# Sixteen rows of zeros on the store queue ahead of a streaming L1 normalisation

## The chip, the core and the metric

The kernel runs on one core of one Trainium2 chip. The metric is device time in microseconds (us), the median of repeated executions; lower is better. Engines are named as in the profile: DVE is VectorE, ACT is ScalarE, POOL is GpSimd, SP is SyncE, PE is TensorE (not used here). "q1" is the DMA queue on which SP issues transfers, "q10" the one on which ACT issues them.

## What is computed

Each row of 1024 floats is divided by the sum of its absolute values plus a tiny constant. There are 32 x 512 = 16384 rows, 67.1 MB in and as much out.

```python
def setup_inputs():
    batch, seq, dim = 32, 512, 1024
    return {"x": np.random.randn(batch, seq, dim).astype(np.float32)}

def reference(x):
    sums = np.sum(np.abs(x), axis=-1, keepdims=True)
    return (x / (sums + 1e-8)).astype(np.float32)
```

## The kernel before

The input is seen as 16384 rows of 1024 elements, and cut into eleven tiles (the list `rows`, line 34). A tile lies over 128 partitions, with twelve rows in each partition (48 KB of a partition, 6 MB in all); the last tile has eight rows per partition (32 KB, 4 MB in all). The function `piece` (lines 36 to 43) says where a tile lies in memory: tiles 0, 1 and the last one share the first 4096 rows of the tensor, 32 consecutive rows per partition, of which tile 0 has the first twelve, tile 1 the next twelve and the last tile the last eight. Tiles 2 to 9 are blocks of 1536 consecutive rows.

Tiles live in a pool of four buffers (`BUFS`, line 45), so that up to four are in flight. The result is written over the input in the same buffer, and stored from there. A second pool, `stats`, holds the row sums and their reciprocals.

For each tile the loop (lines 86 to 91) does the following. SP issues the load (line 88). DVE reduces the absolute values along each row (line 52), adds the constant (line 59) and takes the reciprocal (line 61). Then the rows are multiplied: most of them by one DVE multiplication with the reciprocal broadcast (line 63), in a few tiles some rows by single DVE instructions (line 70) and some by ACT (line 73). The table `split` says how many rows go to the second and third way. Last, ACT issues the store of the tile (line 91). There are eleven loads on q1 and eleven stores on q10.

The body stands in a manual schedule: every engine executes its own instructions in the order in which the program writes them, and the framework adds the semaphore waits that the data call for. A load into a buffer waits until the store that used this buffer before has landed; so load 4 waits for store 0. On SP there is nothing but loads, on ACT multiplications and stores alternate, and on DVE each tile's instructions follow those of the tile before.

Of the kernel before, what the change touches and what calls it, by code (L numbers as in the profile page):

```python
# [1 line left out]

# [4 lines left out]

FP32 = mybir.dt.float32
EPS = 1e-8


@with_exitstack
def kernel(
    ctx: ExitStack,
    tc: tile.TileContext,
    x: bass.AP,
    out: bass.AP,
):
    nc = tc.nc
    P = nc.NUM_PARTITIONS  # L20

    x_flat = x.flatten_outer_dims()
    out_flat = out.flatten_outer_dims()
    n, d = x_flat.shape

    R = 12
    BUFS = 4  # L30
    HEAD = 32
    per_partition = n // P
    assert n % P == 0 and (per_partition - HEAD) % R == 0
    rows = [R] * ((per_partition - HEAD) // R + 2) + [HEAD - 2 * R]

    def piece(flat, i):
        head = flat[: P * HEAD, :].rearrange("(p r) d -> p r d", p=P)
        if i < 2:
            return head[:, R * i : R * (i + 1), :]
        if i == len(rows) - 1:  # L40
            return head[:, 2 * R :, :]
        a = P * (HEAD + R * (i - 2))
        return flat[a : a + P * R, :].rearrange("(p r) d -> p r d", p=P)

    sbuf = ctx.enter_context(tc.tile_pool(name="sbuf", bufs=BUFS))
    stats = ctx.enter_context(tc.tile_pool(name="stats", bufs=len(rows)))

    def normalize(x_tile, k, kv, kt):


        s = stats.tile([P, R], FP32)
        nc.vector.tensor_reduce(  # L52
            out=s[:, :k],
            in_=x_tile[:, :k, :],
            axis=mybir.AxisListType.X,
            op=mybir.AluOpType.add,
            apply_absolute_value=True,
        )
        nc.vector.tensor_scalar_add(out=s[:, :k], in0=s[:, :k], scalar1=EPS)  # L59
        inv = stats.tile([P, R], FP32)  # L60
        nc.vector.reciprocal(out=inv[:, :k], in_=s[:, :k])  # L61
        if kv:
            nc.vector.tensor_mul(  # L63
                out=x_tile[:, :kv, :],
                in0=x_tile[:, :kv, :],
                in1=inv[:, :kv].unsqueeze(2).to_broadcast([P, kv, d]),
            )
        for r in range(kv, kv + kt):
            row = x_tile[:, r, :]
            nc.vector.tensor_scalar_mul(out=row, in0=row, scalar1=inv[:, r : r + 1])  # L70
        for r in range(kv + kt, k):
            row = x_tile[:, r, :]
            nc.scalar.activation(  # L73
                out=row,
                in_=row,
                func=mybir.ActivationFunctionType.Copy,
                scale=inv[:, r : r + 1],
            )

    last = len(rows) - 1
    split = {0: (3, 4), 1: (0, 3), 2: (0, 3), last - 1: (0, 2), last: (5, 3)}

    with tc.manual_schedule():
        for i, k in enumerate(rows):
            x_tile = sbuf.tile([P, R, d], FP32)
            nc.sync.dma_start(out=x_tile[:, :k, :], in_=piece(x_flat, i))  # L88
            kt, ks = split.get(i, (0, 0))
            normalize(x_tile, k, k - kt - ks, kt)  # L90
            nc.scalar.dma_start(out=piece(out_flat, i), in_=x_tile[:, :k, :])


# [1 line left out]
_INS = ['x']  # L95
_OUTS = [((32, 512, 1024), 'float32')]


# [23 lines left out]
```

## Time and profile before

| | us |
|---|---|
| median of 3 runs | 316.94 |
| lowest and highest | 316.83, 317.59 |
| span of the profiled execution | 315.80 |
| DVE busy in that span | 261.2 (83%) |
| ACT busy | 17.4 (6%) |
| bytes read and written | 67.11 MB each, 425 GB/s over the span |

The profile is of one execution; its span goes from the first to the last instruction on the core, and the page gives that execution no other time. The page divides the span into 40 slices and gives the busy share of each engine in tenths; the line "DMA" there is the mean share of the core's 16 DMA engines. The windows of the trace give the same for any stretch, with the bytes moved. The list of DMA queues can be asked for any stretch too: it then counts the packets that began in it, their megabytes, and the time that these packets took as a share of 16 engines over the stretch, which can so be over 100%. One packet of data is what one partition contributes to a transfer.

The costliest groups of instructions, with count, busy time and mean duration:

| line, engine | what | count | busy us | mean ns |
|---|---|---|---|---|
| 52 DVE | sum of absolute values, 128x12288 | 10 | 129.5 | 12950 |
| 63 DVE | multiplication, 128x12288 | 6 | 77.8 | 12958 |
| 73 ACT | multiplication of one row per partition, 128x1024 | 15 | 16.1 | 1138 |
| 70 DVE | the same on DVE, 128x1024 | 8 | 5.5 | 748 |

A load of 6 MB takes 38.0 us from issue to landing in the median (16.9 for the first, 80.6 at most), a store 47.4 us; the last store, of 4 MB, 20.6 us.

### The profile page before, as it was taken

Reading aid. Unit: us, or ns where it says so; the run is one execution under the profiler, and the core shown is the slowest. Engines: PE = TensorE matmul, PEld = TensorE weight load, DVE = VectorE, ACT = ScalarE, POOL = GpSimd, SP = SyncE. Lnnn points to the kernel's source line nnn. Section 1 sums busy time; section 2 is a strip of 40 time slices with the busy share of each in tenths; the row PEclk is TensorE's granted clock in tenths of the full one; section 3 lists DMA queues with packets and bytes.
Section 4 is the critical chain, followed back from the end, with each engine's and each line's share of the span. In section 5 each row is a group of like instructions: output and inputs, shape, how many; then the busy total and the mean of one; then the engine's idle time right before and its main releaser. Section 6 shows DMA issues by size and latency. Waiting matters only on the chain.

```text
span 315.8 us, 168 instructions
## 1 busy us (share of the span) xinstructions
DVE 261.2 (83%) x51; ACT 17.4 (6%) x16; POOL 0.2 (0%) x4
## 2 busy tenths in 40 slices
DVE  0079999999999999969996999799699969999200
ACT  0010404004000000000000000000000000201200
POOL 0000000000000000000000000000000000000000
DMA  8999999999999999999999999999999999999986
GB/s 324 473 398 448 448 361 430 405 486 405 405 486 405 405 486 411 423 467 405 448 436 411 479 405 411 473 417 405 473 417 411 467 413 450 421 442 423 473 374 282
DMA packets 3168, 134.22 MB, mean 425 GB/s; under 512 B 352, under 2 KB 352, under 8 KB 352
## 3 DMA queue, kind: packets, MB, share of 16 engines
q1 hardware_dynamic: 1584, 67.11, 49.8%
q10 hardware_dynamic: 1584, 67.11, 49.1%
HBM read 67.11 MB, written 67.11 MB: 425 GB/s over the span
## 4 chain that ended last, share of the span: by engine, by line
DVE 41%; DMA 33%; another core or an unknown queue 18%; issue 0%; SPq 0%; DVEq 0%
DVE s L52 23%; DMA x_tile<-in_x_dram 17%; DMA out_dram<-x_tile 16%; DVE x_tile L63 15%; DVE x_tile L70 1%; DVE inv L61 0%; DVE s L59 0%; SPq L88 0%; DVEq L117 0%
## 5 line engine op out<-in xcount | busy, mean ns | idle before, releaser
L52 DVE TENSOR_REDUCE s<-x_tile 128x12 f32<-128x12288 f32 (+1 forms) x11 | 138.2, 12561 | 31.5 <-DMA x_tile<-in_x_dram 31.5
L63 DVE TENSOR_TENSOR x_tile<-x_tile,inv 128x12288 f32<-128x12288 f32 (+3 forms) x10 | 113.6, 11358 | 0.5
L73 ACT ACTIVATE x_tile<-x_tile,inv 128x1024 f32<-128x1024 f32 x15 | 16.1, 1138 | 258.7 <-DVE inv L61 258.7
L70 DVE TENSOR_SCALAR x_tile<-x_tile,inv 128x1024 f32<-128x1024 f32 x8 | 5.5, 748 | 0.0
L61 DVE RECIPROCAL inv<-s 128x12 f32<-128x12 f32 (+1 forms) x11 | 2.5, 226 | 0.4
L73 ACT ACT_TABLE_LOAD x1 | 1.3, 1283 | 17.7 <-DMA x_tile<-in_x_dram 17.7
L59 DVE TENSOR_SCALAR s<-s 128x12 f32<-128x12 f32 (+1 forms) x11 | 1.9, 173 | 0.4
L106 POOL MEMSET const-bfloat16-1.0<- 128x1 bf16 x1 | 0.1, 102 | 0.0
L106 POOL MEMSET const-uint8-127<- 128x1 uint8 x1 | 0.1, 102 | 0.0
L106 POOL MEMSET const-float32-0.0<- 128x1 f32 x1 | 0.1, 99 | 0.2 <-issue 0.2
L106 POOL MEMSET const-float32-1.0<- 128x1 f32 x1 | 0.1, 99 | 0.0
## 6 DMA issues: line engine op xcount, KB each, us to landing
x_tile<-in_x_dram SPq DMA_DIRECT2D x10, 6144.0 KB, 38.0
out_dram<-x_tile ACTq DMA_DIRECT2D x10, 6144.0 KB, 47.4
x_tile<-in_x_dram SPq DMA_DIRECT2D x1, 4096.0 KB, 33.3
out_dram<-x_tile ACTq DMA_DIRECT2D x1, 4096.0 KB, 20.6
```

Of the source, the lines that this page charges most:

```text
L52: nc.vector.tensor_reduce(out=s[:, :k], in_=x_tile[:, :k, :], axis=mybir.AxisListType.X, op=mybir.AluOpType.add, apply_absolute_value=True,)
L59: nc.vector.tensor_scalar_add(out=s[:, :k], in0=s[:, :k], scalar1=EPS)
L61: nc.vector.reciprocal(out=inv[:, :k], in_=s[:, :k])
L63: nc.vector.tensor_mul(out=x_tile[:, :kv, :], in0=x_tile[:, :kv, :], in1=inv[:, :kv].unsqueeze(2).to_broadcast([P, kv, d]),)
L70: nc.vector.tensor_scalar_mul(out=row, in0=row, scalar1=inv[:, r : r + 1])
L73: nc.scalar.activation(out=row, in_=row, func=mybir.ActivationFunctionType.Copy, scale=inv[:, r : r + 1],)
L106: nc = _bacc.Bacc("TRN2", target_bir_lowering=False, num_devices=1)
```

## The change

A small tile of zeros, 16 partitions of 128 floats, is filled by DVE, and ACT issues a transfer that writes it to the result: 512 bytes into the beginning of 16 different rows, the first row of the last tile in each of its first 16 partitions. The last tile's store writes all of these places again at the end. The loop is rewritten into functions for load, computation and store; the first four loads are written ahead of the loop, and load i + 4 behind store i.

```diff
+    tiles = {}
+
+    def load(i):
+        x_tile = tiles[i] = sbuf.tile([P, R, d], FP32, name="x_tile")
+        nc.sync.dma_start(out=x_tile[:, : rows[i], :], in_=piece(x_flat, i))
+
+    def store(i):
+        nc.scalar.dma_start(out=piece(out_flat, i), in_=tiles[i][:, : rows[i], :])
+
+    def compute(i):
+        k = rows[i]
+        kt, ks = split.get(i, (0, 0))
+        normalize(tiles[i], k, k - kt - ks, kt)
+
     with tc.manual_schedule():
-        for i, k in enumerate(rows):
-            x_tile = sbuf.tile([P, R, d], FP32)
-            nc.sync.dma_start(out=x_tile[:, :k, :], in_=piece(x_flat, i))
-            kt, ks = split.get(i, (0, 0))
-            normalize(x_tile, k, k - kt - ks, kt)
-            nc.scalar.dma_start(out=piece(out_flat, i), in_=x_tile[:, :k, :])
+        zero = ctx.enter_context(tc.tile_pool(name="zero", bufs=1)).tile([16, 128], FP32, name="zero")
+        nc.vector.memset(zero, 0.0)
+        nc.scalar.dma_start(out=piece(out_flat, len(rows) - 1)[:16, 0, :128], in_=zero)
+        for i in range(BUFS):
+            load(i)
+        for i in range(len(rows)):
+            compute(i)
+            store(i)
+            if i + BUFS < len(rows):
+                load(i + BUFS)
```

## The prediction

> **What bounds the kernel now.** I read the busy slices first, then the table of windows, the waits and the timeline, and last the DMA queues in single microseconds.
>
> ```profile
> DVE  0079999999999999969996999799699969999200
> DMA  8999999999999999999999999999999999999986
> q1 hardware_dynamic: 1584, 67.11, 49.8%
> q10 hardware_dynamic: 1584, 67.11, 49.1%
> ```
>
> The 16 DMA engines are busy in every slice; VectorE starts late and has holes. q1 (SP's loads) and q10 (ACT's stores) share those engines half and half. Of 3168 packets 352 are under 512 B (completion marks), so 2816 carry data, 176 per engine: 160 of 48 KB (a partition's twelve rows) and 16 of 32 KB (eight rows).
>
> ```profile
> 120.00:140.00 20.00, 18.04 (x4) 0.00 (x0) 0.00 (x0) 1.00 1.00 435
> 40.00:60.00 20.00, 19.90 (x4) 3.23 (x3) 0.00 (x0) 1.00 1.02 415
> 0.00:2.00 2.00, 0.00 (x0) 0.00 (x0) 0.20 (x4) 1.00 1.10 344
> ```
>
> The columns are window, length, busy DVE, ACT and POOL, clock, DMA share and GB/s. The rate is 435 in the middle and 415 in the window in which the first store joins: 20 GB/s for 20 us is 0.40 MB, or 0.9 us of transfer lost there.
>
> ```profile
> DVE s L52 <- DMA x_tile<-in_x_dram: 31.5, 7, 17.6
> 140.72 12.95 DVE L52 TENSOR_REDUCE s<-x_tile 128x12 f32<-128x12288 f32 x1 [2.51 <-DMA x_tile<-in_x_dram]
> 38.67 0.38 ACTq L91 DMA_DIRECT2D out_dram<-x_tile  x1
> ```
>
> VectorE waits for loads, 17.6 us before the first and some 2.5 us before each of the later ones; nobody waits long for VectorE except ACT, whose share is small. So the end is set by how much work each DMA engine has, and by nothing else that I can find. The third row is the first store: issued at 38.67 us, the first use of q10.
>
> The single microseconds show where the 0.9 us went. A packet is counted where it starts and the share is of 16 engines, so share x 16 / packets is the duration of one.
>
> ```profile
> q1 hardware_dynamic: 14, 0.69, 220.9%
> ...
> q1 hardware_dynamic: 16, 0.79, 181.5%
> ...
> q1 hardware_dynamic: 15, 0.74, 170.6%
> ...
> q1 hardware_dynamic: 16, 0.79, 307.9%
> ...
> q10 hardware_dynamic: 15, 0.74, 170.2%
> ```
>
> These are the microseconds from 1, 4, 38, 40 and 43. The very first packets take 2.209 x 16 / 14 = 2.52 us. Later ones take 1.815 us (1.815 x 16 / 16), and those of 38 us 1.82. At 40 us, just before q10's first packets start, one packet on every engine takes 3.079 us: 1.26 us too long. q10's first packets themselves (43 us) take 1.815. Both queues hold work from then on (a load takes 38.0 us to land and the next is issued after some 29), so no row shows what a restart after a pause would cost. **The stall of 1.26 us per engine belongs to q10's first use, and it falls where the engines have no slack.** Check of the sum: 160 x 1.815 + 16 x 1.21 (by bytes) = 309.8; plus 1.7 us before the first packet, 0.70 for the long first packets and 1.26 for the stall gives 313.5, beside a span of 315.8 in which the transfers die out in the 314th microsecond.
>
> **The change part by part.** All sums stand against the span of 315.80; the median of the runs is 316.94, 1.14 us more, and I carry that over unchanged, since the page gives the profiled execution no time of its own.
>
> *The order of the Python loop: 0.* Loads, computation and stores are now written as functions, and four loads come ahead of the loop. SP issues nothing but loads, in the same order, each still behind the store that frees its buffer; VectorE and ACT keep their orders too. Loads 0 to 3 already leave together in the trace (SP's four issues span 0.73 to 2.62 us). Load 4 leaves at 74.08 because store 0 (38.67 + 35.3) has landed by then, and it still must.
>
> *The memset: 0 to 0.2 us, hidden.* POOL's memsets of 128x1 take 0.10 us, VectorE's add on 128x12 0.17. VectorE has nothing to do until 17.65 us; that wait hides it. Without this cover it would cost 0.2 us once. Queued behind it on ACT is only the zero store, for which it must wait; what is next on ACT waits for load 0 at 17.70 us anyway.
>
> *The 16 rows of zeros: 0.02 us per engine by their bytes.* If the rows are spread over the engines, each gets 512 B, and 512 / 49152 x 1.815 = 0.02 us. The other end is one whole packet's time, 1.8 us, if an engine is held as long by a small packet as by a large one. I take the small end, since the rate follows bytes in all rows above, and keep the other for the range.
>
> [...]
>
> *The last store must come after the zeros: 0.* Only store 10 overwrites them, at 294.08 us. The zeros should land within some microseconds of the start, so an added wait on ACT is long met; queued behind it is nothing but the end. Were the wait put on store 0 at 38.67 it would be met as well.
>
> *The first use of q10 moves to the head: from -1.26 to +1.26 us.* When does it come? Load 0 is issued at 0.73 and its first packets start in the microsecond from 1, by the 2-us window around 1.7: about 1.0 us of lag. The zero store can be issued after the memset, 0.73 + 0.2, so by the same lag q10's rows reach the engines at about 1.9 us. There the engines do no full work: the first q1 packets run 2.52 - 1.82 = 0.70 us longer than normal. If q10's start is served in that waiting time, 0.70 of the 1.26 is hidden in any case, and all of it if it begins before data flows. The gain then lies between 0.70 - 0.02 = 0.68 and 1.26 - 0.02 = 1.24; I take the middle, 1.0.
>
> [...] The trace's own lag of 1.0 us is what I use.
>
> What is late next? If the head loses up to 1.26 us, load 0 and VectorE's start move from 17.65 to at most 18.9. VectorE runs without a gap until 111.17, then waits 0.57 us for load 4 and 2.51 us before the reduction at 140.72. A delay of 1.26 us is gone by that second wait, and q10 is never empty meanwhile (store 2, issued at 84.92, takes 47.1 us, and store 3 leaves at 111.19). VectorE passes nothing of it on.
>
> **The rivals.**
>
> *Forecast, the stall is hidden at the head:* 316.94 - 1.0 = 315.9. For it: the stall is seen once, and the engines wait at the head anyway. Against it: at 40 us q1 had packets waiting and could not fill the stall, so an engine may stop as a whole.
>
> *The stall only moves:* engines stop 1.26 us at about 4 us, when load 0's first packets are through, instead of at 40. -1.26 + 1.26 + 0.02 gives 316.96, no change. It decides if the zeros reach the engines after load data flows, which is 0.2 us away by my working. For it: the same argument about whole engines.
>
> *The stall is not prepaid (slower):* it belongs to the first large store, not to the queue, and stays at 40 us; the zeros pay one more at the head. +1.26 + 0.02 gives 318.2. It is decided by what a 512 B packet leaves behind in an engine. For it: no row shows a small packet preparing a large one, and neither queue has a pause after its start in which a cost of restarting could be seen. Against it: both queues go over 67 MB of new addresses afterwards with packets of 1.815, so it isn't new addresses that cost the time.
>
> *The change does nothing at all* (an ordering wait holds the zeros back until late): then q10 starts at 38.67 as before and the time is 316.94; it goes with the second case.
>
> **How the numbers follow.** Hidden at the head 0.43, moved or without effect 0.33, not prepaid 0.24. A difference of 0.3% is 0.95 us, about what measurement can tell from no change: 315.99 and 317.89 are the marks. The first case holds gains from 0.68 to 1.24 and is on the faster side in most of its span; a few partial gains fall to "same" and a few from the second case come out faster. So faster 0.41, same 0.35, slower 0.24. The time is that of the likeliest case, 315.9; its own range is 315.6 to 316.3. The range goes from 315.4 (the whole 1.24 and the 0.3 us by which repeated runs differ) to 318.1, which holds nearly all of the second case and part of the third.
>
> **What would show it.** In the changed kernel's trace the packets of the 40th microsecond should take 1.815 us and not 3.08; the window from 40 to 60 should reach some 435 GB/s; q10's first packets should stand near 2 us, the load packets after them should take 2.5 us and no more, and VectorE should start at 17.65 or at most 0.5 later. If packets near 4 us take 3 us and VectorE starts near 18.9, the stall has moved. If 3.08 is still there at 40 us, it was not prepaid. The prediction is wrong if the stall has another cause than q10's first use, or if small packets hold an engine for a microsecond.

## The result and the profile after

The changed kernel takes 317.78 us in the median of 20 runs, beside 317.22 us for 20 runs of the kernel before: a ratio of 1.0016, 95% interval 1.001 to 1.0023. It is slower by 0.56 us in the medians, some 0.2%. Compared once more (12 and 23 runs) it gave 317.57 beside 317.20, ratio 1.0015 (0.9999 to 1.0031), an interval that just reaches 1. The forecast was 1.0 us faster.

The page of the changed kernel, with its two new rows:

```profile
span 316.1 us, 170 instructions
DVE  0079999999999999969996997899699969999100
DMA  8999999999999999999999999999999999999986
q1 hardware_dynamic: 1584, 67.11, 49.7%
q10 hardware_dynamic: 1616, 67.12, 49.0%
L96 DVE MEMSET zero<- 16x128 f32 x1 | 0.2, 165 | 0.8 <-PEq L119 0.8
out_dram<-zero ACTq DMA_DIRECT2D x1, 8.0 KB, 7.5
```

The picture is the old one. q10 has 32 packets more, 16 of zeros and, between 7 and 9 us, 16 of under 512 B, as many as each of the 22 transfers has in the page of before (352); the zeros land 7.5 us after their issue. The stretches and the waits that the prediction read, in the changed kernel's windows, its waits and its timeline:

```profile
40.00:60.00 20.00, 19.90 (x4) 3.23 (x3) 0.00 (x0) 1.00 1.02 413
120.00:140.00 20.00, 17.73 (x4) 0.00 (x0) 0.00 (x0) 1.00 1.00 435
...
DVE s L47 <- DMA x_tile<-in_x_dram: 29.9, 7, 16.6
...
38.65 0.36 ACTq L85 DMA_DIRECT2D out_dram<-x_tile  x1
```

The window in which the first store joins still moves 413 GB/s beside 435 (415 before). VectorE starts at 17.62 us (17.65 before) and the first store leaves at 38.65 (38.67). Now the DMA queues of the changed kernel in the microseconds from 1, from 4, from 5 to 7 (two rows), from 40 and from 43; again the share x 16 x the window's length / packets is one packet's time:

```profile
q1 hardware_dynamic: 15, 0.74, 235.9%
...
q1 hardware_dynamic: 16, 0.79, 181.5%
...
q1 hardware_dynamic: 16, 0.79, 90.8%
q10 hardware_dynamic: 16, 0.01, 1.4%
...
q1 hardware_dynamic: 16, 0.79, 309.8%
...
q10 hardware_dynamic: 15, 0.74, 170.2%
```

The zeros run from 5 to 7 us, each for 1.4% x 16 x 2 / 16 = 0.03 us, and the load packets beside them take the normal 1.816. At 40 us the packets take 309.8% x 16 / 16 = 3.10 us, as they did before (3.08). **The stall was neither prepaid nor moved, and q10's first use shows no cost in the packets.** So the transfer explains no gain, and the loss has to be looked for elsewhere.

The loss is in two other places. The first is the close of the program, where all five engines have drains and semaphore waits. These are the rows of the generated closing code from 314.6 us on, four of each kernel, first in the kernel before, then in the changed one (engine, count, duration in ns, first and last start):

```profile
L117 SPq DRAIN  x3: 7/7/7, 314.9 to 315.2; - x3
L117 DVEq EVENT_SEMAPHORE  x2: 21/21/21, 315.1 to 315.8; - x2
L117 ACTq DRAIN  x1: 8/8/8, 315.2 to 315.2; - x1
L117 DVEq DRAIN  x1: 19/19/19, 315.3 to 315.3; - x1
```

```profile
L130 SPq DRAIN  x3: 7/7/7, 315.0 to 315.3; - x3
L130 DVEq EVENT_SEMAPHORE  x2: 21/21/21, 315.2 to 316.1; - x2
L130 ACTq DRAIN  x1: 8/8/8, 315.3 to 315.3; - x1
L130 DVEq DRAIN  x1: 143/143/143, 315.8 to 315.8; - x1
```

Before, VectorE drains at 315.3 us, with ScalarE, and only its very last wait is late: the trace has it at 315.78 us, where the other engines have theirs at 315.59 to 315.60. In the changed kernel the drain itself comes at 315.76, 0.44 us behind ScalarE's (315.32), and the others wait for it: the last waits of SyncE and ScalarE come at 316.05 and 316.06. From SyncE's drain ahead of the closing barriers (the second of its three) to the end it is 0.82 us before (314.98 to 315.80) and 1.05 us in the changed kernel (315.07 to 316.12): 0.23 us. In both kernels 0.52 us pass between the starts of the 63rd and the 64th row that VectorE has in the trace, its waits and drains counted. Before, the 64th row is the last wait; in the changed kernel it is the drain, which otherwise follows its predecessor after 0.11 us.

The second place is outside the span. Every run lists its time and its span. Time less span is 1.62 us (1.58 to 1.68) over the kernel before's runs beside the first four experiments, and 1.78 us (1.74 to 1.81) over the changed kernel's 20. The ranges don't touch: 0.16 us more. With 0.23 that is 0.39 us, inside the interval of the measured loss (0.1% to 0.23% of 317.2 us, 0.3 to 0.7 us). The second comparison has the spans of both kernels side by side: the median span is 315.8 us beside 315.6, the median time less span 1.77 beside 1.61, and the two differences make up its 0.37 us.

### The profile page after: what moved, and what is told of

Its sections match the earlier page's. It is cut to its first block, busy times and chain, and to the rows that moved or that the text cites. A ratio compares the mean times of both kernels' runs of the same rounds, so it can differ in the third digit from the quotient of the medians.

```text
span 316.1 us, 170 instructions
## 1 busy us (share of the span) xinstructions
DVE 261.4 (83%) x52; ACT 17.4 (6%) x16; POOL 0.2 (0%) x4
## 4 chain that ended last, share of the span: by engine, by line
DVE 41%; DMA 33%; another core or an unknown queue 18%; SPq 0%; issue 0%; DVEq 0%
DVE s L47 23%; DMA x_tile<-in_x_dram 17%; DMA out_dram<-x_tile 16%; DVE x_tile L58 15%; DVE x_tile L65 1%; DVE inv L56 0%; DVE s L54 0%; SPq L82 0%; DVEq L130 0%
```

## The experiments

**Theory A.** The memset is one more VectorE instruction, and its place in the count of instructions, not its 0.17 us of work, costs the time: VectorE's stream pauses (the 0.52 us above) at a fixed place in the count, and the memset pushes that place from ahead of the last wait to ahead of the last drain. Rival B: the transfer of the zeros costs it. Rival C: the rewritten loop, with another order of semaphores, costs it. The first four runs take the change apart. They were timed together, with 35 runs of the kernel before (317.45 us).

*The loop alone.* Edit against the changed kernel:

```diff
-        zero = ctx.enter_context(tc.tile_pool(name="zero", bufs=1)).tile([16, 128], FP32, name="zero")
-        nc.vector.memset(zero, 0.0)
-        nc.scalar.dma_start(out=piece(out_flat, len(rows) - 1)[:16, 0, :128], in_=zero)
```

> The loop rewritten into functions, without the zeros and without their memset: one part of the change alone. Theory A (the closing barrier waits about 0.5 us for VectorE, because one more VectorE instruction moves the place at which its instruction stream pauses): VectorE has as many instructions as before, so the span is 315.8 us as before (316.1 in the changed kernel) and the last VectorE drain comes within 0.05 us of those of the other engines; time ratio to before 1.000. Rival B (the zero transfer itself delays the DMA engines): also 315.8. Rival C (the new order of allocation and of semaphores costs it): 316.1, ratio 1.0016.

Measured: ratio 1.0007 (0.9998 to 1.0016), span 316.0, from SyncE's drain to the end 0.84 us, VectorE's drain on time (0.03 us behind ScalarE's), time less span 1.63. The close is that of before; the span's extra 0.2 us is in the transfers, which end 0.2 us later in this execution. Rival C is not needed, but within this interval not excluded for a part. The runs with the GpSimd memset below keep the rewritten loop and come to 0.9997 and 1.0002, which leaves little for it.

*The memset alone, no transfer.* The loop is that of the changed kernel. Here and below an edit is against the changed kernel unless another is named.

```diff
-        nc.scalar.dma_start(out=piece(out_flat, len(rows) - 1)[:16, 0, :128], in_=zero)
```

> As the changed kernel, with the memset on VectorE but without the transfer of the zeros. Theory A: span 316.0 to 316.2 us, VectorE's last drain at about 0.5 us behind ScalarE's as in the changed kernel; ratio about 1.001. Rival B (the transfer costs it): span 315.8, drain on time, ratio 1.000.

Measured: ratio 1.0011 (1.0002 to 1.002), span 316.2. The late drain is back without any zeros being written: VectorE's at 315.88, ScalarE's at 315.45, 1.05 us from SyncE's drain to the end; time less span 1.78. The closing rows of this kernel:

```profile
L129 ACTq DRAIN  x1: 8/8/8, 315.4 to 315.4; - x1
L129 DVEq DRAIN  x1: 143/143/143, 315.9 to 315.9; - x1
```

*The zeros written, but filled by GpSimd.*

```diff
-        nc.vector.memset(zero, 0.0)
+        nc.gpsimd.memset(zero, 0.0)
```

> As the changed kernel, with the memset of the zeros on GpSimd in place of VectorE; the zeros are written. Theory A: VectorE's stream is that of before, its last drain is on time, span 315.8 to 315.9 us, ratio 1.000 (0.9995 to 1.0007). Rival B (the transfer costs it): span 316.1, ratio 1.0016. Both: the 1.26 us stall of the q1 packets of the 40th microsecond is still there (308% of 16 engines in that microsecond).

Measured: ratio 0.9997 (0.9988 to 1.0006), span 315.9, 0.82 us from SyncE's drain to the end, time less span 1.64. The transfer is there and costs nothing that can be measured. Rival B falls. The packets of 40 us take 2.98 us here. The closing rows:

```profile
L130 ACTq DRAIN  x1: 8/8/8, 315.3 to 315.3; - x1
L130 DVEq DRAIN  x1: 19/19/19, 315.3 to 315.3; - x1
```

*Eight memsets, no transfer.* If the instructions' own work cost time, this would be the slowest.

```diff
-        nc.vector.memset(zero, 0.0)
-        nc.scalar.dma_start(out=piece(out_flat, len(rows) - 1)[:16, 0, :128], in_=zero)
+        for _ in range(8):
+            nc.vector.memset(zero, 0.0)
```

> Eight memsets of the zero tile on VectorE in place of one, no transfer of the zeros. Theory A: the pause of VectorE's instruction stream moves eight instructions forward, into the last tile's work or its wait for the last store to land, where nothing waits for it; the last drain and the last semaphore of VectorE are on time and the span is 315.6 us, 0.2 below before (before has the pause ahead of its very last instruction). Rival (each VectorE instruction simply costs time, or the closing differs from run to run): 316.1 or more.

Measured: ratio 1.0002 (0.9992 to 1.0012), span 315.6 as expected. VectorE's drain and its last wait are both on time, 0.67 us from SyncE's drain to the end, the shortest of the four. Time less span stays at 1.80. The 64th row of VectorE is now the first single-row multiplication of the last tile, and the pause stands there. Its timeline row in the changed kernel, where it comes 0.22 us behind the row before it, and in this one, where it comes 0.50 us behind:

```profile
290.02 2.08 DVE L65 TENSOR_SCALAR x_tile<-x_tile,inv 128x1024 f32<-128x1024 f32 x3
...
290.31 2.08 DVE L65 TENSOR_SCALAR x_tile<-x_tile,inv 128x1024 f32<-128x1024 f32 x3 [0.31 <-DVE inv L56]
```

*Two memsets in the changed kernel, zeros written.*

```diff
         nc.vector.memset(zero, 0.0)
+        nc.vector.memset(zero, 0.0)
```

> The changed kernel with the memset of the zeros done twice on VectorE: one VectorE instruction more than the changed kernel, and the zeros are written as there. Theory A (VectorE's instruction stream has a pause of about 0.5 us at a fixed count of instructions, and the changed kernel puts it between the two closing barriers' waits): the pause moves one more instruction ahead, to where VectorE waits for the last store anyway; the drain is on time, the span is 315.6 to 315.8 us, ratio 0.999 to 1.0005, so the kernel with more work is 0.4 us faster than the changed one. Rival (VectorE's extra instructions cost time themselves, or the zero transfer does): 316.1 to 316.3, ratio 1.0016 or more.

Measured: ratio 1.0004 (0.9987 to 1.0021), 317.32 us beside 317.49. The profiled execution's span is 315.8, and the median of all its spans is 315.5 beside 315.9 for the kernel before in the same job. 0.67 us from SyncE's drain to the end, time less span 1.78. One instruction more than the changed kernel takes the late drain away; the interval is too wide to call it faster than the changed kernel by the clock alone. The closing rows:

```profile
L131 ACTq DRAIN  x1: 8/8/8, 315.4 to 315.4; - x1
L131 DVEq DRAIN  x1: 24/24/24, 315.4 to 315.4; - x1
```

*The changed kernel and the GpSimd memset once more, in one job.*

> The changed kernel itself, timed beside the next one and with the same runs of the kernel before. Theory A accounts for 0.23 us of the closing barrier (0.82 us from SyncE's drain to the end before, 1.05 in the changed kernel): ratio 1.0007, with what else there may be up to 1.0016. If the first comparison's 1.0016 holds, at least 0.2 us comes from elsewhere.

> The zeros filled by GpSimd once more. Theory A: VectorE's closing drain on time, ratio 0.9995 to 1.0003, and 0.2 us or more below the changed kernel of the same job. Rival (the zeros or their place in the queue cost it): as the changed kernel.

Measured: 1.0015 (0.9999 to 1.0031) and 1.0002 (0.9992 to 1.0012). 1.05 and 0.84 us from SyncE's drain to the end; time less span 1.77 and 1.64. Both repeat.

Ordered by the number of rows that VectorE has in the trace, its waits among them, the runs so far are:

| VectorE rows | kernels | SyncE's drain to the end, us | time less span, us | ratio |
|---|---|---|---|---|
| 64 | before, loop alone, GpSimd memset (twice) | 0.82 to 0.84 | 1.62 to 1.64 | 1, 1.0007, 0.9997, 1.0002 |
| 65 | changed (twice), memset alone | 1.05 | 1.77 to 1.78 | 1.0016, 1.0015, 1.0011 |
| 66, 72 | two memsets, eight memsets | 0.67 | 1.78 to 1.80 | 1.0004, 1.0002 |

From 64 to 65 rows the close grows by 0.23 us and the part outside the span by 0.16; with more rows the pause leaves the close, which shrinks by 0.15 against before, while the 0.16 outside stays.

**What the stall at 40 us is.** The next runs ask whose it is, since it isn't q10's first use by a small transfer.

*Store 0 on q1, no zeros.* The three lines of the zeros are left out, in this run and the next two; of the edit only the rest is shown. All other stores stay on q10.

```diff
-        nc.scalar.dma_start(out=piece(out_flat, i), in_=tiles[i][:, : rows[i], :])
+        queue = nc.sync if i == 0 else nc.scalar
+        queue.dma_start(out=piece(out_flat, i), in_=tiles[i][:, : rows[i], :])
```

> No zeros. Store 0 is issued by SyncE on q1 instead of by ScalarE on q10; all other stores stay on q10, so q10 is first used by store 1 at about 62 us. Theory Q (the stall belongs to the first full-sized transfer of a queue): packets of 40 us take 1.82 us, and a stall of about 1.26 us per engine is found near 63 us. Rival W (it belongs to the first large write to the result, whatever the queue): about 1.26 us more at or shortly after 40 us (as soon as q1 comes to store 0), nothing at 63 us. Rival M (it belongs to the two directions mixing): a stall where loads and stores first alternate. The time itself may grow by a few us, since q1 then takes turns between loads and a store in order.

Measured: ratio 0.9994 (0.9984 to 1.0004), span 315.3. The rows of 40, 58 and 66 us:

```profile
q1 hardware_dynamic: 16, 0.79, 181.5%
...
q1 hardware_dynamic: 16, 0.79, 274.2%
...
q10 hardware_dynamic: 9, 0.44, 102.1%
```

Nothing stalls at 40 us. The last packets of load 3, at 58 us, take 2.74 us, 0.93 too long, just before q1 comes to store 0. q10's first use, store 1 at 66 us, has packets of 1.815 and none beside it is stretched. The stall goes with the first large write, not with the queue: theory Q falls, W stands, with a smaller size than it was given. For rival M, the mixing of the two directions, this run has a second place: from 61 to 95 us only stores run, on both queues, and when the loads come back at 95 us the packets on either side of the change take 1.815. So not every change of direction brings a stall.

*Load 1 on q10, no zeros.*

```diff
-        nc.sync.dma_start(out=x_tile[:, : rows[i], :], in_=piece(x_flat, i))
+        queue = nc.scalar if i == 1 else nc.sync
+        queue.dma_start(out=x_tile[:, : rows[i], :], in_=piece(x_flat, i))
```

> No zeros. Load 1 is issued by ScalarE on q10 at the start, all other loads by SyncE on q1, all stores on q10: q10's first use is a full-sized load at the start. Theory Q: the stall moves to the first microseconds or vanishes there, the packets of 40 us take 1.82 us; span 314.6 if it vanishes, 315.8 if it only moves. Rival W (first large write): 3.08 us packets stay at about 40 us and the span is 315.8.

Measured: ratio 1.0151 (1.0119 to 1.0183), 321.82 us, which I had not expected. Load 0 now shares the engines with load 1, so VectorE starts at 32.44 us and not at 17.6; the first store leaves at 53.47. q10 has been used by a large load since the start, and still the packets of 55 us, ahead of the first store's, take 274.3% x 16 / 16 = 2.74 us. That again is as W has it.

*A large transfer of zeros* in place of the 512-byte rows. 16 x 32 KB, one packet per engine, from the buffer of load 3 before it is loaded; GpSimd fills it.

```diff
+        if i == BUFS - 1:
+            nc.gpsimd.memset(x_tile[:16, :8, :], 0.0)
+            nc.scalar.dma_start(out=piece(out_flat, len(rows) - 1)[:16, :8, :], in_=x_tile[:16, :8, :])
         nc.sync.dma_start(out=x_tile[:, : rows[i], :], in_=piece(x_flat, i))
```

> In place of the 16 x 512 B of zeros, 16 x 32 KB of zeros (one packet per engine) from the buffer of load 3, filled by GpSimd before load 3, written on q10 to places that the last store overwrites. Theories Q and W: the stall comes with this transfer, within the first 20 us, and the packets of 40 us take 1.82 us; the time is that of before plus 1.2 us for the bytes, 318.1 us, less whatever of the stall is hidden. Rival M (two streams of large packets in opposite directions, at every new start): 3.08 us packets appear both with this transfer and at 40 us; 319.4 us.

Measured: ratio 1.0059 (1.0031 to 1.0088), 318.31 us. The profiled execution is one of the two long ones (321.29 us; the other five lie between 318.2 and 318.9). The rows of 42 and 44 us:

```profile
q1 hardware_dynamic: 15, 0.74, 184.3%
...
q1 hardware_dynamic: 14, 0.69, 175.0%
```

They are 1.97 and 2.00 us per packet, 0.15 and 0.19 too long: some 0.3 us is left of the stall at the first store. Summed over the packets between 8 and 17 us, 0.7 us per engine of excess is found near the zeros' own packets. So after a write large enough little of the stall is left at the first store, but 0.7 us is paid at the write's own place, where the engines are as busy (shares of 1.13 and 0.99 in the two windows from 8 to 16 us, 0.94 and 0.98 from 40 to 48), and its bytes come on top. This kernel's VectorE has 66 rows, by two more waits; its close is short (0.69 us) and its time less span 1.80, as the table has it.

*16 rows of 4096 bytes, filled by GpSimd.*

```diff
-        zero = ctx.enter_context(tc.tile_pool(name="zero", bufs=1)).tile([16, 128], FP32, name="zero")
-        nc.vector.memset(zero, 0.0)
-        nc.scalar.dma_start(out=piece(out_flat, len(rows) - 1)[:16, 0, :128], in_=zero)
+        zero = ctx.enter_context(tc.tile_pool(name="zero", bufs=1)).tile([16, d], FP32, name="zero")
+        nc.gpsimd.memset(zero, 0.0)
+        nc.scalar.dma_start(out=piece(out_flat, len(rows) - 1)[:16, 0, :], in_=zero)
```

> The zeros as 16 rows of 4096 bytes in place of 512, filled by GpSimd. If the stall is prepaid in proportion to what is written first (512 B left 1.28 us at 40 us, 32 KB per engine left 0.3): something between, 0.9 to 1.2 us at 40 us, span 315.8. If a few KB are enough: 0.3 at 40 us and up to 0.75 in the first 10 us, span 315.0 to 315.8. If only the change of direction of a long stream counts: 1.26 stays, span 315.9.

Measured: ratio 1.0 (0.9983 to 1.0016). The profiled execution is its longest (span 318.3; the median of its spans is 315.65). The excess over 1.815 us per packet is 0.94, 0.21 and 0.03 us per engine in the pairs of microseconds from 40, 42 and 44, 1.18 in all, about as in the changed kernel (1.24 in its second profile, 1.30 in its first). Eight times the bytes prepay nothing that this spread would show.

*Both gains together:* store 0 on q1, and two memsets of an unused tile on VectorE. The edit against the run with store 0 on q1:

```diff
+        zero = ctx.enter_context(tc.tile_pool(name="zero", bufs=1)).tile([16, 128], FP32, name="zero")
+        nc.vector.memset(zero, 0.0)
+        nc.vector.memset(zero, 0.0)
```

> No zeros written. Store 0 on q1 as in the run with store 0 on q1 (span 315.3), and two memsets of an unused tile on VectorE, which move its pause away from the closing barrier: theory A 315.1 us in the span, ratio 0.9985 to 0.9995, below both kernels. If the two effects don't add, 315.3 to 315.6.

Measured: ratio 0.9998 (0.9982 to 1.0015), span 316.4 in the profiled execution, 315.6 in the median. A miss: it doesn't beat the kernel before by anything that can be measured. The close is 0.67 us as expected and the stall, at 58 us, 0.89 us, but the transfers of that execution end at 315.1 us, 1.4 us later than in the run with store 0 on q1, without longer packets; why is open. Time less span is 1.79, so 0.16 us of the gain at the close is given back there.

## Why the prediction was wrong

The reading of the bound was right: the transfers set the end, with 3.08 us packets at 40 us as the one visible loss among them. Three steps failed.

*"The stall of 1.26 us per engine belongs to q10's first use."* This failed first, and with it the forecast. It stood on one event with two firsts in it, the first use of a queue and the first large write. Store 0 on q1 separated them: the stall went with the write (2.74 us packets at 58 us), and q10's first use had none. The third rival named this, "it belongs to the first large store, not to the queue, and stays at 40 us", and was right in that half. Its other half, a second stall at the head for +1.26, didn't come: packets of 512 B took 0.03 us, and the load packets next to them 1.816.

*"... by the same lag q10's rows reach the engines at about 1.9 us."* They were issued at 1.01 us, as reckoned (0.93), but ran between 5 and 7 us, behind two load packets on each engine. The covering time of 0.70 us at the head was over by then. Had the stall been q10's, by the prediction's own condition it would have moved and not been hidden.

*"The memset: 0 to 0.2 us, hidden."* This is the step that gave the wrong sign. Its work was hidden, its place in the instruction stream was not: 0.23 us in the closing barriers and 0.16 us outside the span. The wait for load 0 (16.65 us) covered the memset's 0.17 us and not its place in the count. With it failed a term that the sum held fixed: the time outside the span, which it took as 1.14 us and carried over "unchanged". By each run's own time and span it is 1.62 us before and 1.78 after.

That 317.78 lies inside the stated range of 315.4 to 318.1 is luck: the range is built from what the stall may do, and the loss is none of that.

Right were 0 for the order of the loop within what runs can tell, 0 for the last store's wait, and 0.02 us per engine for the zeros by their bytes (0.03 measured). What was long was the landing of the 8 KB, 7.5 us, which nobody waited for.

Two things stay open. What the engines do during the stall ahead of the first large write isn't shown, only when it comes, that 32 KB per engine leave 0.3 us of it and that 4 KB leave 1.18 us, about the whole.

The other is what VectorE's pause is. The traces show one thing beside it that moves with VectorE's rows: each of the 14 has exactly one packet of the kind "instruction" after its start, of 8 KB. In the ten with 64 or 65 VectorE rows it begins 0.64 to 0.77 us behind the 64th row, after the end of the span; in the four with 66 or 72 it lies inside, at 294 to 304 us. The DMA queues of the microsecond from 316 in the changed kernel, and of that from 294 in the run with eight memsets:

```profile
q14 instruction: 1, 0.01, 3.3%
...
q14 instruction: 1, 0.01, 1.9%
```

That this packet has to do with VectorE is inferred from its moving with VectorE's rows. It isn't what VectorE waits for: it begins after the pause, and in the microsecond from 315, where the changed kernel pauses, the trace records no DMA packet. Nor does the packet explain the 0.16 us outside the span, which stay with 66 and 72 rows, where it lies inside the span.

## What to carry to other kernels

When one event in a trace is the first of two kinds, find a run that separates them before building on either; here a change of two lines, store 0 on the other queue, did it. A difference of 0.1% or 0.2% in a kernel bound by transfers can sit in the close of the program and outside its span, as here, so read the closing rows of each engine, and time less span, before explaining it by the part that was changed. The memset lay in a wait of its engine, and its kernel was still 0.2% slower than before, while with the memset on GpSimd it was not (0.9997 and 1.0002): try the same work on another engine before calling an instruction free.

## What was not expected of the hardware

VectorE has a pause at a fixed place in its instruction stream, the 64th row of its trace in all kernels here. From the 63rd row's start to the 64th's it is 0.50 to 0.54 us in the eleven runs in which that row doesn't wait for the last store; at other places the same instructions come 0.11 us (drain), 0.22 us (multiplication) and some 0.35 us (last wait) behind their predecessors. With 64 rows it delays only the last wait, with 65 the closing barrier (0.23 us), with 66 and 72 nothing that is waited for. Time less span is in the medians 1.61 to 1.66 us with 64 rows and 1.77 to 1.80 us with more.

In all runs but the one with the large zeros, the first store after the opening loads comes with a stretched packet before it on the 16 engines, from 1.815 to between 2.65 and 3.13 us in the mean, whichever queue it is on. In the run with load 1 on q10, where only stores ran from some 64 to 81 us, the return of the loads did something alike: q10's packets of 79 us took 2.56 us, and q1's first ones at 81 us 2.87 us. In the run with store 0 on q1 the loads' return at 95 us did not; what makes the difference is open.
